# Hard-max attention on one core: key-group gathers in twos and one tile sooner throughout the loop, value gathers caught up from the sixteenth tile on

## The chip, the core and the metric

The kernel runs on one core of one Trainium2 chip. The metric is the time of one execution on the device, in microseconds (us); smaller is better. Engines are named as in the profile: PE (TensorE matmul), PEld (its weight load), DVE (VectorE), ACT (ScalarE), POOL (GpSimd), SP (SyncE). "L229" is line 229 of the kernel before.

## What is computed

```python
B, Sq, Sk, D = 4, 4096, 4096, 128
logits = np.matmul(q, k.transpose(0, 2, 1))
best = np.argmax(logits, axis=-1)
return v[b_idx, best, :]          # the value row of the best key, for every query
```

There is no softmax: each of the 16,384 query rows takes the one value row whose key has the largest product with it.

## The kernel before

**Tiles.** A tile is 128 query rows; there are 128 tiles (T = 128), 32 to a batch (NQT = 32). Iteration `it` of the main loop issues work for several tiles at different stages, and the program order of the loop is the order on each engine, since the schedule is manual.

**The screen (PE, ACT, DVE).** Keys are taken in groups of four, 1024 groups to a batch. `screen` makes four 128x1024 products in PSUM with half-precision sums and differences of keys: `dpart` (L203) has ACT take an absolute value, `spart` (L213) adds it back on PE, and ACT writes one half as E (L216). `fold` (L229) merges E with the other half on DVE into W, an integer score per group with the group's number in its low bits, and `top` (L233) takes the eight largest of 1024 on DVE. In this text the fold is called W and the max M, as their tiles W and TOP are the easiest to find in the rows. A tile costs DVE one W and one M.

**The group gather (DVE, POOL).** `gather` (L245, tile `cand`) decodes the best group's number of some tiles on DVE, and puts one indirect DMA per tile into the queue `near_q`; POOL issues it (L251, tile `kg`): it fetches the differences of the four keys of the best group, 384 half-precision numbers a row. `issue`, at the end of each iteration, takes one entry of `near_q` (two near the end).

**The dots (DVE).** `dots` waits until all gathers of its group of tiles have been issued, and some iterations more, and then multiplies kg by the query (L269, `prod`), halves the sum twice (L274 and L277, tiles `p1` and `p2`, both shown as `p`) and reduces it (L279, `D`). `pick` (L289 to L302: `mx`, `near`, `sel`, `CNT`, `win`) chooses the key for a chunk of eight tiles (four near the end).

**The value gather (POOL, SP).** `put_values` queues four indirect DMAs in `late_q`; POOL issues them (L309, tile `vr`), one or two an iteration by `take_late`, and SP stores them (L314).

**The flagged rows.** Rows whose screen was too close to call are counted and redone exactly for half of the tiles at a time: by `flag_segment` (L325 to L442) in between the loop's work from tile 64 on, and by `flags_first` and `flags_last` (L447 to L540) at the end. The last part has a branch on the count, which is not taken here.

**What sets the order.** `start` puts a generator into the list `live`; `step`, called twice an iteration, advances each by one DVE instruction: a `dots` only within a quota (one a step, two where two are waiting), a `pick` or flags generator by one. In the loop of before, an iteration is: screen, W of the tile before, `step`, M of the tile before that, `gathers` for the tile three back (from iteration TAIL = 104 on: two back), `step`, `issue`. `gathers` makes groups of four tiles for tiles 0 to 71, of two for 72 to 125, and of one for the last two. NKG is the number of kg buffers, each for four tiles.

The call that decides all of it is short:

```python
        step(it)
        if it >= 2:
            top(it - 2)
        if 3 <= it <= TAIL:
            gathers(it - 3)
        if it >= TAIL:
            gathers(it - 2)
        step(it)
        issue(it)
```

Of the kernel before, what the change touches and what calls it, by code (L numbers as in the profile page):

```python
# [8 lines left out]
FP16 = mybir.dt.float16  # L9
# [6 lines left out]
OP = mybir.AluOpType  # L16
# [5 lines left out]
TAU = 8.0  # L22
NEAR = 0.5
LATE = 7
NKG = 6


@with_exitstack
def kernel(ctx, tc, q, k, v, out):
    nc = tc.nc  # L30
    B, Sq, D = q.shape
    Sk = k.shape[1]
    P = 128
    NQT = Sq // P
    T = B * NQT
# [12 lines left out]
    rp = ctx.enter_context(tc.tile_pool(name="ref", bufs=2))  # L48
# [12 lines left out]
    natq = [bp.tile([P, NQT, P], FP16, name=f"natq{i}", tag=f"natq{i}") for i in range(2)]  # L61
# [65 lines left out]
    iota_h = cp.tile([P, P], FP16, tag="iota_h")  # L127
# [93 lines left out]
    def screen(t):  # L221
        dpart(t, 0)
        spart(t - 1, 0)
        dpart(t, 1)
        spart(t - 1, 1)
# [9 lines left out]
    fast, near_q, late_q = [], [], []  # L235
    kg_t, cand_t = {}, {}
    done, stores, marks = set(), set(), set()
    wait_q = []

    def gather(c, t0, n):  # L240
        c0, c1 = chunks[c]
        if t0 == c0:
            cand_t[c] = sp.tile([P, c1 - c0], U32, tag=f"cand{c1 - c0}", name=f"cand_{c}", bufs=6)
        x = cand_t[c][:, t0 - c0:t0 - c0 + n]
        nc.vector.tensor_scalar(out=x, in0=TOP.bitcast(U32)[:, t0:t0 + n, 0], scalar1=IDX, scalar2=IDX,  # L245
                                op0=OP.bitwise_and, op1=OP.bitwise_xor)
        kg = rp.tile([P, 4, 3, P], FP16, tag="kg", name=f"kg_{t0}", bufs=NKG)[:, 0:n]
        assert len(kg_t) < NKG
        kg_t[t0] = kg
        for j in range(n):  # L250
            near_q.append(lambda j=j: nc.gpsimd.indirect_dma_start(  # L251
                out=kg[:, j].rearrange("p f d -> p (f d)"), out_offset=None, in_=k16[t0 // NQT],
                in_offset=IOA(ap=x[:, j:j + 1], axis=0)))
        mark = lambda: done.add(("kg", t0))
        marks.add(mark)
        near_q.append(mark)
        start(dots(c, t0, n), "dots", c)

    def dots(c, x, m):
        c0 = chunks[c][0]  # L260
        d = D_t[c % 4]
        b = x // NQT
        gap = ("wait", 1) if m == 4 else ("dve",)
        yield "until", lambda: ("kg", x) in done, 2 if m < 4 and x < TAIL else 1
        kg = kg_t.pop(x)
        prod = rp.tile([P, 4, 3, P], FP16, tag="prod", name=f"prod_{x}")[:, 0:m]
        h = min(m, 2)
        for i in range(0, m, h):
            nc.vector.tensor_tensor(out=prod[:, i:i + h], in0=kg[:, i:i + h],  # L269
                                    in1=natq[b % 2][:, x + i - b * NQT:x + i + h - b * NQT, :].unsqueeze(2).to_broadcast([P, h, 3, P]),  # L270
                                    op=OP.mult)
            yield gap
        p1 = rp.tile([P, 4, 3, 64], FP16, tag="p1", name=f"p1_{x}")[:, 0:m]
        nc.vector.tensor_tensor(out=p1, in0=prod[:, :, :, 0:64], in1=prod[:, :, :, 64:128], op=OP.add)  # L274
        yield gap
        p2 = rp.tile([P, 4, 3, 32], FP16, tag="p2", name=f"p2_{x}")[:, 0:m]
        nc.vector.tensor_tensor(out=p2, in0=p1[:, :, :, 0:32], in1=p1[:, :, :, 32:64], op=OP.add)  # L277
        yield "dve",
        nc.vector.tensor_reduce(out=d[:, x - c0:x - c0 + m, 1:4], in_=p2, axis=AX_X, op=OP.add)  # L279
        done.update(("dot", i) for i in range(x, x + m))  # L280
# [40 lines left out]
    def put_rec(t0, t1):  # L321
        nc.sync.dma_start(out=rec.rearrange("(p t) w -> p t w", t=T)[:, t0:t1, :], in_=TOP.bitcast(U32)[:, t0:t1, :])
# [3 lines left out]
    def flag_segment(t0, t1, ready, stored):  # L326
# [40 lines left out]
        posn = fp.tile([P, 8], FP16, tag="posn", name=f"posn_{t0}")  # L367
        nc.vector.scalar_tensor_tensor(out=posn, in0=iota_r[:, 0:8], scalar=bs, in1=val, op0=OP.add, op1=OP.mult)
        yield "dve", 0.17
        OH = fp.tile([P, 8, P], BF16, tag="OH", name=f"OH_{t0}")  # L370
        nc.vector.tensor_tensor(out=OH, in0=iota_h.unsqueeze(1).to_broadcast([P, 8, P]),
                                in1=posn.unsqueeze(2).to_broadcast([P, 8, P]), op=OP.is_equal)
        yield "dve", 0.17
        rec2 = fp.tile([P, 8, 2], BF16, tag="rec2", name=f"rec2_{t0}")
        nc.vector.tensor_copy(out=rec2[:, :, 0], in_=e8)
        yield "dve", 0.17
# [241 lines left out]
    live = []  # L618

    def start(g, kind, c=None):  # L620
        live.append({"g": g, "kind": kind, "c": c, "wake": 0, "until": None, "n": 0})

    def ready(s, it):
        if s["until"] is not None:
            if not s["until"]():
                return False
            s["until"], s["wake"] = None, it + s["n"]
        return it >= s["wake"]

    def advance(s, it, free):  # L630
        if not (ready(s, it) or free and s["until"] is None):
            return False
        try:
            y = next(s["g"])
        except StopIteration:
            live.remove(s)
            return True
        if y[0] == "wait":
            s["wake"] = it + y[1]
        elif y[0] == "until":  # L640
            s["until"], s["n"] = y[1], y[2]
            return advance(s, it, free)
        return True

    def step(it):
        quick = it >= TAIL
        waiting = [s for s in live if s["kind"] == "dots" and ready(s, it)]
        quota = 2 if len(waiting) > 1 else 1
        for s in list(live):
            if s["kind"] == "dots":  # L650
                if quota and advance(s, it, False):
                    quota -= 1
            else:
                if advance(s, it, False) and quick and s["kind"] == "pick" and s in live:
                    advance(s, it, False)

    rest = [0]
# [1 line left out]
    def take_late(n):  # L659
        while n > 0 and late_q:  # L660
            g = late_q.pop(0)
            n -= g not in stores
            g()
        while late_q and late_q[0] in stores:
            wait_q.append((clock[0] + 2, late_q.pop(0)))
# [3 lines left out]
    def put_out(now):  # L669
        while wait_q and wait_q[0][0] <= now:  # L670
            wait_q.pop(0)[1]()

    def issue(it):
        n = 0
        clock[0] = it
        put_out(it)
        while near_q and (n < 1 + (it >= T - 28 and len(near_q) > 2) or near_q[0] in marks):
            g = near_q.pop(0)
            n += g not in marks
            g()  # L680
        if fast and it >= rest[0]:
            fast.pop(0)()
            rest[0] = it + 3
        take_late(2 if n == 0 and len(late_q) > 4 or it >= T - 24 and it % 2 == 0 else 1)

    def gathers(t):
        for c, (t0, t1) in enumerate(chunks):
            m = 4 if t1 <= T - 56 else 2 if t < T - 2 else 1
            if t0 <= t < t1 and (t - t0) % m == m - 1:
                gather(c, t - m + 1, m)  # L690
            if t == t0:
                start(pick(c, t0, t1), "pick", c)
        if t % 8 == 7:
            put_rec(t - 7, t + 1)
        if t == SEGS[1] - 1:
            last = [c for c, x in enumerate(chunks) if x[1] == t + 1][0]
            start(flag_segment(0, t + 1, lambda: ("cnt", last) in done, lambda: ("out", last) in done), "flags")

    TAIL = T - 24
    units = []  # L700
    for b in range(1, B):
        x = b * NQT
        units += [(x - 1, x - NQT + (6 + 3 * i // 2 if b == 1 else 1 + 2 * i), unit_k, b, i) for i in range(16)]
    for it in range(T):
        b, qt = it // NQT, it % NQT
        if it < 8:
            load_part(1, it)
        elif 10 <= qt < 18:
            load_part(b + 1, qt - 2)
        elif 18 <= qt < 26:  # L710
            load_part(b + 2, qt - 18)
        open_units = [u for u in units if u[1] <= it]
        if open_units:
            u = min(open_units)
            units.remove(u)
            assert it <= u[0]
            u[2](*u[3:])
        if it == 1:
            turn_q(0, 4, 8)
        if it in (1, 2, 3):  # L720
            turn_q(0, it * 8, it * 8 + 8)
        elif qt >= 16 and qt % 2 == 0 and b + 1 < B:
            turn_q(b + 1, (qt - 16) * 2, (qt - 14) * 2)
        if it > 0:
            screen(it)
        if it >= 1:
            fold(it - 1)
        if it == 1:
            put_k(0, 1)
        if it % NQT in (9, 13):  # L730
            put_k(it // NQT + 1, it % NQT // 13)
        step(it)
        if it >= 2:
            top(it - 2)
        if 3 <= it <= TAIL:
            gathers(it - 3)
        if it >= TAIL:
            gathers(it - 2)
        step(it)
        issue(it)  # L740

    def flush():
# [73 lines left out]
```

## Time and profile before

| what | value |
|---|---|
| three executions | 461.14, 462.56, 462.96 us; median 462.56 us |
| the profiled execution | 462.96 us; its span in the trace 461.1 us |
| busy share of the span | DVE 90%, PE 82%, ACT 82%, POOL 68% |
| DVE W (L229) | 128 instructions, 166.0 us |
| DVE M (L233) | 128 instructions, 156.2 us |
| DVE dots (L269, L274, L277, L279) | 65, 47, 47, 47 instructions |
| POOL gathers (L251 and L309) | 128 each, 125.7 and 134.7 us |

The span runs from the first to the last recorded instruction; the 1.9 us between it and the execution's time lie outside the trace. A record's length is not what an instruction costs its engine in a busy stretch: on DVE and ACT the next record often starts before the last one has ended. The distance from one start to the next is called the pitch here, and it is what adds up.

### The profile page before, as it was taken

To read this page: it belongs to the slowest core of one execution; us is meant where nothing else is said; L and a number is where in the kernel's file an instruction comes from. 1 tells how busy PE (TensorE), PEld (TensorE's weight loads), DVE (VectorE), ACT (ScalarE), POOL (GpSimd) and SP (SyncE) were. 2 spreads that over 40 slices of the span, in tenths; PEclk is the share of its full clock that TensorE was granted. 3 is DMA by queue.
4 is the path that set the end of the run, shared out by engine and by line. 5 is a ranking of instruction groups with operands and counts; after the bars stand their busy time and mean duration, and the time that the engine had idled before them with its cause. 6 is when DMAs were issued, how large, how long until landed. Compare 5 with 4: busy or idle time off the path is not lost. (4 is left out here: it accounts for less than half of the span.)

```text
span 461.1 us, 6319 instructions
## 1 busy us (share of the span) xinstructions
PE 380.2 (82%) x1834; PEld 168.1 (36%) x1834; DVE 414.6 (90%) x758; ACT 376.3 (82%) x437; POOL 314.3 (68%) x345
## 2 busy tenths in 40 slices
PE   8999999999998899989998889998988888850100
PEld 4444444444443344444443344433333333320100
DVE  2689999999999999899999999999999999989430
ACT  2999999999999999999999898999998887750000
POOL 8304556777667878877768877667777777777730
PEclk9999999999999999999999999999999999995555
DMA  7934657473335877843346842613333332332320
GB/s 127 199 85 96 131 91 121 76 117 86 85 97 117 163 140 113 150 95 89 88 125 139 135 122 76 132 35 83 102 104 99 87 106 78 86 94 78 96 77 4
DMA packets 43625, 47.54 MB, mean 103 GB/s; under 512 B 25001, under 2 KB 33452, under 8 KB 43585
## 3 DMA queue, kind: packets, MB, share of 16 engines
q0 software_dynamic: 18752, 30.97, 33.3%
q1 hardware_dynamic: 24832, 16.13, 13.8%
q8 instruction: 14, 0.23, 0.2%
q14 instruction: 27, 0.21, 0.2%
HBM read 39.59 MB, written 12.19 MB: 112 GB/s over the span
## 5 line engine op out<-in xcount | busy, mean ns | idle before, releaser
L203 ACT ACTIVATE A<-pd 128x1024 f16<-128x1024 f32 x256 | 259.4, 1043 | 20.5 <-PE pd L194 20.0
L251 POOL DMA_INDIRECT kg<-k,cand x128 | 125.7, 982 | 80.5 <-DVE cand L245 45.2
L229 DVE SCALAR_TENSOR_TENSOR W<-psn,E 128x1024 int16<-128x1024 f32 x128 | 166.0, 1297 | 7.8 <-ACT E L216 6.6
L194 PE MATMUL psn<-kT,qT 128*128 128x512 f16 x512 | 151.9, 378 | 16.3 <-ACT A L203 7.1
L194 PE MATMUL pd<-kT,qT 128*128 128x512 f16 x512 | 151.8, 378 | 13.0 <-ACT A L203 11.3
L309 POOL DMA_INDIRECT vr<-in_v_dram,win x128 | 134.7, 1053 | 40.3 <-issue 35.6
L194 PEld LDWEIGHTS <-qT 128*128 128x128 f16 x1024 | 98.0, 97 | 162.5 <-issue 74.3
L233 DVE MAX8 TOP<-W 128x8 f32<-128x1024 f32 x128 | 156.2, 1220 | 0.0
L213 PE MATMUL psn<-A,identh 128*128 128x512 f16 x512 | 152.1, 378 | 0.0
L216 ACT ACTIVATE E<-psn 128x1024 int16<-128x1024 f32 x128 | 132.3, 1033 | 4.2 <-PE psn L213 4.2
L213 PEld LDWEIGHTS <-identh 128*128 128x128 f16 x512 | 49.6, 97 | 60.8
L269 DVE TENSOR_TENSOR prod<-kg,natq 128x768 f16<-128x768 f16 (+1 forms) x65 | 35.3, 543 | 3.0 <-DMA kg<-k,cand 3.0
L174 ACT ACTIVATE kT<-uk 128x256 f16<-128x256 f32 x48 | 20.4, 424 | 1.4 <-PE uk L171 1.4
L274 DVE TENSOR_TENSOR p<-prod 128x384 f16<-128x384 f16 (+2 forms) x47 | 20.0, 426 | 0.1
L279 DVE TENSOR_REDUCE D<-p 128x6 f32<-128x192 f16 (+2 forms) x47 | 19.7, 419 | 0.1
L65 POOL DMA_DIRECT2D natk<-in_k_dram x27 | 16.0, 600 | 0.8 <-POOLq L800 0.8
L68 POOL DMA_DIRECT2D natq<-in_q_dram x27 | 16.2, 603 | 0.0
L170 PE MATMUL uk<-identh,natk 128*128 128x128 f16 x96 | 15.8, 218 | 0.0
L469 PE MATMUL fp_e<-n_e,tri 128*128 128x1 f32 x2 | 0.6, 362 | 16.4 <-DVE n_e L467 16.4
L277 DVE TENSOR_TENSOR p<-p 128x192 f16<-128x192 f16 (+2 forms) x47 | 13.5, 287 | 0.1
L171 PEld LDWEIGHTS <-natk 128*128 128x128 f16 x96 | 9.3, 97 | 7.0 <-issue 4.5
L170 PEld LDWEIGHTS <-natk 128*128 128x128 f16 x96 | 9.4, 98 | 5.6
(147 smaller groups left out, 131.5 us busy)
## 6 DMA issues: line engine op xcount, KB each, us to landing
out_dram<-vr SPq DMA_DIRECT2D x32, 256.0 KB, 2.2
natq<-in_q_dram POOLq DMA_DIRECT2D x26, 128.0 KB
k<-kd SPq DMA_DIRECT2D x8, 384.0 KB, 2.9
natk<-in_k_dram POOLq DMA_DIRECT2D x24, 128.0 KB
kg<-k,cand POOLq DMA_INDIRECT x128
vr<-in_v_dram,win POOLq DMA_INDIRECT x128
natq<-in_q_dram POOLq DMA_DIRECT2D x1, 768.0 KB
natk<-in_k_dram POOLq DMA_DIRECT2D x1, 512.0 KB
```

Source lines behind the costliest of these rows:

```text
L170: nc.tensor.matmul(out=o, lhsT=natk[b % 2][:, h, 4 * m + x, :], rhs=identh, start=True, stop=False)
L174: nc.scalar.activation(out=kT[b % 2][:, c:c + 256], in_=ps, func=AF.Copy)
L194: nc.tensor.matmul(out=ps[:, n * 512:(n + 1) * 512], lhsT=qT[b % 2][:, qt * P:(qt + 1) * P], rhs=kT[b % 2][:, u * 1024 + n * 512:u * 1024 ...
L203: nc.scalar.activation(out=A, in_=ps, func=AF.Abs)
L213: nc.tensor.matmul(out=ps[:, n * 512:(n + 1) * 512], lhsT=identh, rhs=A[:, n * 512:(n + 1) * 512], start=False, stop=True)
L216: nc.scalar.activation(out=E, in_=ps, func=AF.Relu, scale=QSCALE)
L229: nc.vector.scalar_tensor_tensor(out=W_t[t % NW].bitcast(I16)[:, 1::2], in0=ps, scalar=QSCALE, in1=E, op0=OP.mult, op1=OP.max)
L233: nc.vector.max(out=TOP[:, t, :], in_=W_t[t % NW].bitcast(FP32))
L251: near_q.append(lambda j=j: nc.gpsimd.indirect_dma_start(out=kg[:, j].rearrange("p f d -> p (f d)"), out_offset=None, in_=k16[t0 // NQT], ...
L269: nc.vector.tensor_tensor(out=prod[:, i:i + h], in0=kg[:, i:i + h], in1=natq[b % 2][:, x + i - b * NQT:x + i + h - b * NQT, :].unsqueeze(2 ...
L274: nc.vector.tensor_tensor(out=p1, in0=prod[:, :, :, 0:64], in1=prod[:, :, :, 64:128], op=OP.add)
L309: late_q.append(lambda j=j: nc.gpsimd.indirect_dma_start(out=vr[:, j, :], out_offset=None, in_=v_flat, in_offset=IOA(ap=win[:, i + j:i + j ...
```

## The change

The change does seven things, all in the order of the work: (1) groups are of two tiles for tiles 0 to 125, with eight kg buffers of two tiles in place of six of four; (2) `gathers` always works two tiles back, and after the second `step` in place of before it; (3) `dots` yields as "dve" alone, and waits two iterations after its gathers up to TAIL, one from there on; TAIL is 90 in place of 104; (4) `issue` takes two entries of `near_q` wherever more than three wait; (5) `issue` takes a second value gather wherever more than eight wait and it is every third iteration (and when more than three wait with no group gather taken, or in the last 28 iterations); (6) a flags generator is advanced twice a step, and picks twice from the new TAIL on; (7) the one-hot comparison of `flag_segment` is cut into four instructions, an iteration apart.

```diff
-NKG = 6
...
-        kg = rp.tile([P, 4, 3, P], FP16, tag="kg", name=f"kg_{t0}", bufs=NKG)[:, 0:n]
-        assert len(kg_t) < NKG
+        kg = rp.tile([P, 2, 3, P], FP16, tag="kg", name=f"kg_{t0}", bufs=8)[:, 0:n]
+        assert len(kg_t) < 8
...
-        gap = ("wait", 1) if m == 4 else ("dve",)
-        yield "until", lambda: ("kg", x) in done, 2 if m < 4 and x < TAIL else 1
+        yield "until", lambda: ("kg", x) in done, 1 if x >= TAIL else 2
...
-        h = min(m, 2)
-        for i in range(0, m, h):
-            nc.vector.tensor_tensor(out=prod[:, i:i + h], in0=kg[:, i:i + h],
...
-            yield gap
+        nc.vector.tensor_tensor(out=prod, in0=kg, in1=natq[b % 2][:, x - b * NQT:x - b * NQT + m, :].unsqueeze(2).to_broadcast([P, m, 3, P]),
+                                op=OP.mult)
+        yield "dve",
...
-        nc.vector.tensor_tensor(out=OH, in0=iota_h.unsqueeze(1).to_broadcast([P, 8, P]),
-                                in1=posn.unsqueeze(2).to_broadcast([P, 8, P]), op=OP.is_equal)
-        yield "dve", 0.17
+        for z in range(4):
+            nc.vector.tensor_tensor(out=OH[:, 2 * z:2 * z + 2], in0=iota_h.unsqueeze(1).to_broadcast([P, 2, P]),
+                                    in1=posn[:, 2 * z:2 * z + 2].unsqueeze(2).to_broadcast([P, 2, P]), op=OP.is_equal)
+            yield "wait", 1
...
-                if advance(s, it, False) and quick and s["kind"] == "pick" and s in live:
+                if advance(s, it, False) and (quick or s["kind"] == "flags") and s in live:
...
-        while near_q and (n < 1 + (it >= T - 28 and len(near_q) > 2) or near_q[0] in marks):
+        behind = len(near_q) > 3
+        while near_q and (n < 1 + behind or near_q[0] in marks):
...
+            n += 1
-        take_late(2 if n == 0 and len(late_q) > 4 or it >= T - 24 and it % 2 == 0 else 1)
+        left = len([g for g in late_q if g not in stores])
+        more = n == 0 and left > 3 or n < 2 and it % 3 == 0 and left > (8 if it < T - 28 else 3)
+        take_late(2 if more else 1)
...
-            m = 4 if t1 <= T - 56 else 2 if t < T - 2 else 1
+            m = 2 if t < T - 2 else 1
...
-    TAIL = T - 24
+    TAIL = T - 38
...
         step(it)
         if it >= 2:
             top(it - 2)
-        if 3 <= it <= TAIL:
-            gathers(it - 3)
-        if it >= TAIL:
+        step(it)
+        if it >= 2:
             gathers(it - 2)
-        step(it)
         issue(it)
```

More of the change, by code (lines that the diff above doesn't have):

```diff
@@ L262, in dots @@
         b = x // NQT
-        gap = ("wait", 1) if m == 4 else ("dve",)
-        yield "until", lambda: ("kg", x) in done, 2 if m < 4 and x < TAIL else 1
+        yield "until", lambda: ("kg", x) in done, 1 if x >= TAIL else 2
         kg = kg_t.pop(x)
-        prod = rp.tile([P, 4, 3, P], FP16, tag="prod", name=f"prod_{x}")[:, 0:m]
-        h = min(m, 2)
-        for i in range(0, m, h):
-            nc.vector.tensor_tensor(out=prod[:, i:i + h], in0=kg[:, i:i + h],
-                                    in1=natq[b % 2][:, x + i - b * NQT:x + i + h - b * NQT, :].unsqueeze(2).to_broadcast([P, h, 3, P]),
-                                    op=OP.mult)
-            yield gap
-        p1 = rp.tile([P, 4, 3, 64], FP16, tag="p1", name=f"p1_{x}")[:, 0:m]
+        prod = rp.tile([P, 2, 3, P], FP16, tag="prod", name=f"prod_{x}")[:, 0:m]
+        nc.vector.tensor_tensor(out=prod, in0=kg, in1=natq[b % 2][:, x - b * NQT:x - b * NQT + m, :].unsqueeze(2).to_broadcast([P, m, 3, P]),
+                                op=OP.mult)
+        yield "dve",
+        p1 = rp.tile([P, 2, 3, 64], FP16, tag="p1", name=f"p1_{x}")[:, 0:m]
         nc.vector.tensor_tensor(out=p1, in0=prod[:, :, :, 0:64], in1=prod[:, :, :, 64:128], op=OP.add)
-        yield gap
-        p2 = rp.tile([P, 4, 3, 32], FP16, tag="p2", name=f"p2_{x}")[:, 0:m]
+        yield "dve",
+        p2 = rp.tile([P, 2, 3, 32], FP16, tag="p2", name=f"p2_{x}")[:, 0:m]
         nc.vector.tensor_tensor(out=p2, in0=p1[:, :, :, 0:32], in1=p1[:, :, :, 32:64], op=OP.add)
```

## The prediction

> **What bounds the kernel now.** First the page's busy shares and its slices. DVE's slices read 9 from the third to the 35th; ACT's and PE's sink to 8 in the last third.
>
> ```profile
> span 461.1 us, 6319 instructions
> PE 380.2 (82%) x1834; PEld 168.1 (36%) x1834; DVE 414.6 (90%) x758; ACT 376.3 (82%) x437; POOL 314.3 (68%) x345
> DVE  2689999999999999899999999999999999989430
> ```
>
> Busy records overlap, so I went on to DVE's timeline and took pitches, from one start to the next. Here are two iterations with groups of four, and two with groups of two:
>
> ```profile
> 105.17 0.16 DVE L245 TENSOR_SCALAR cand<-TOP 128x4 uint32<-128x4 uint32 x1
> 105.22 0.55 DVE L279 TENSOR_REDUCE D<-p 128x12 f32<-128x384 f16 x1
> 105.69 1.30 DVE L229 SCALAR_TENSOR_TENSOR W<-psn,E 128x1024 int16<-128x1024 f32 x1
> 106.88 0.56 DVE L269 TENSOR_TENSOR prod<-kg,natq 128x768 f16<-128x768 f16 x1
> 107.36 1.21 DVE L233 MAX8 TOP<-W 128x8 f32<-128x1024 f32 x1
> 108.50 1.28 DVE L229 SCALAR_TENSOR_TENSOR W<-psn,E 128x1024 int16<-128x1024 f32 x1
> ```
> ```profile
> 302.94 0.26 DVE L245 TENSOR_SCALAR cand<-TOP 128x2 uint32<-128x2 uint32 x1
> 303.00 0.39 DVE L274 TENSOR_TENSOR p<-prod 128x384 f16<-128x384 f16 x1
> 303.27 1.33 DVE L229 SCALAR_TENSOR_TENSOR W<-psn,E 128x1024 int16<-128x1024 f32 x1
> 304.47 0.27 DVE L277 TENSOR_TENSOR p<-p 128x192 f16<-128x192 f16 x1
> 304.63 1.25 DVE L233 MAX8 TOP<-W 128x8 f32<-128x1024 f32 x1
> 305.77 0.36 DVE L279 TENSOR_REDUCE D<-p 128x6 f32<-128x192 f16 x1
> 306.02 1.33 DVE L229 SCALAR_TENSOR_TENSOR W<-psn,E 128x1024 int16<-128x1024 f32 x1
> ```
>
> W takes 1.19 of pitch and M 1.14, whoever follows, and the next record begins some 0.085 before the last one ends. From W of tile 12 (52.16) to W of tile 126 (411.05) the pitches of all of DVE's instructions, each form at its mean, add up to 355.8 of 358.9 us, and three waits below are the other 3.0: DVE is the bound. ACT's own three activations a tile have a pitch of 0.91 each, 2.73, and a kT copy 0.3; a tile of DVE takes 2.92 with groups of four. What interrupts DVE there is one row of the view of waits; the first row is from the start of the loop:
>
> ```profile
> DVE W L229 <- ACT E L216: 6.6, 9, 2.8
> DVE prod L269 <- DMA kg<-k,cand: 3.0, 3, 1.4
> ```
>
> The three waits for kg are 1.40 us at 193, 0.28 at 360 and 1.31 at 407. The last: POOL's gather of that group ended at 406.9, its `prod` began at 408.9, so a gather is usable some 2.0 after its record. In the end part (from W of tile 126 at 411.05) DVE and POOL work through one chain to 461.1.
>
> **The change, part by part.** The built orders of both kernels, side by side, give 75 more DVE instructions and the same number on the other engines. From W of tile 126 on, DVE's order is the same but for one swapped pair, and POOL's from the gather of tile 122 on: the end part does not change. So the sum is over DVE's stretch before it.
>
> *A, groups of two for 72 tiles: +5.2.* A group of four cost prod 2 x 0.467, p1 0.466, p2 0.262, reduction 0.463, cand 0.06 = 2.19. Two groups of two, by the pitches of tiles 72 up, cost 2 x (0.467 + 0.267 + 0.168 + 0.264 + 0.07) = 2.47. 18 groups times 0.28 to 0.30 make 5.0 to 5.4. In the new order cand stands ahead of W, which the trace shows only where W was late anyway (0.18 of pitch); other short ones ahead of W (`near`, `CNT`) cost 0.085 to 0.09, so I keep 0.07 and let 0.18 stretch the range: at most 4 to 5 us more over some 45 such places.
> The Trainium skill, "VectorE: DVE Perf Modes", in the section on the TRN2 errata, speaks against this part: a fixed extra time is paid once per instruction, so large tiles are better than many small ones; its table has 58 cycles at 0.96 GHz, 60 ns, as the fixed part. By that, 72 more instructions would cost an estimated 4.3 in place of 5.2; the rows (p1: 2 x 0.267 - 0.466 = 0.068) win.
>
> *B, the one-hot in four: +0.25.* 1024 elements had a pitch of 1.12 (L371), 512 one of 0.60 (L480); along that line 256 have 0.34, four of them 1.37.
>
> *C, dots sooner: -2.2.* DVE's twelve iterations from W of tile 0 (16.64) to W of tile 12 (52.16) took 35.5, but their pitches add up to 29.6 (12 W, 11 M, two kd of 0.86, two prod, two cand): 5.9 idle, behind ACT's E. In the new order five cand, three prod and three sets of p1, p2 and reduction stand there, 3.0 more work, which is not done later. Stepping through from 34.05 by pitches (3.13 and 2.76 in turn, kd on two of them), never ahead of before's ACT-bound starts, I get W of tile 12 at 52.6 and W of tile 14 0.4 later than before's 58.92. So 3.0 are moved and 0.4 lost; since DVE's lateness also holds ACT's buffers I take 0.8. Bounds: gain 2.8, or none at all, if ACT loses as much as DVE puts in.
>
> *D, cand no longer directly behind its own M: -1.4.* From tile 104 on before works two tiles back, and cand directly behind M started 1.26 after it, not 1.14. Twelve such places, times 0.12. In the new order a `step` stands between; those of the end part stay.
>
> *E, picks and flags two at a time: +1.2.* Where one instruction reads what the last one wrote, its start is 0.035 behind the record's end, not 0.085 ahead: 0.12 each. The built order has ten more such pairs (eight of flags, two of picks).
> On D and E the same page, in "The DRAIN you can't avoid", says that a semaphore between two VectorE operations costs nothing extra. By that rule D and E would both be zero, and the sum 0.2 higher; this trace says otherwise, 1.26 against 1.14.
>
> *F, waits for kg: -3.0 + 1.6.* Before's three go. New ones can come: POOL is in order, pitch 1.26 for a kg and 1.31 for a vr, so an iteration with one of each takes 2.57, a third vr every third iteration 0.43 more, a q or k load 0.61: 3.0 to 3.6 for an iteration of 3.0. While loads run, `prod` stands four iterations behind cand, three whole ones and a W, 10 us, and POOL needs 0.4 + 2 x 1.26 + 2 x 1.31 + 0.6 + 2.0 = 8.1: enough. From tile 90 on it stands three behind. Around tile 106 two flag transfers (FV and the store of its rows) and a second vr stand between the two gathers of a group: 0.4 + 2 x 1.26 + 3 x 1.31 + 2.0 = 8.9 for about 7.8 (two iterations of 3.3 and a W). One to two us there, less than one for the group after. Against that the new order has 52 transfers on POOL between the gathers of tiles 100 and 122, before 58. Bounds: no wait at all, or 4.
>
> *Rest.* SP's queue has the same transfers; transposes of the next batch have over ten iterations of slack. PE and ACT do the same work and have 0.1 to 0.25 a tile to spare. The end part loses one pair of D, -0.1.
>
> *Sum.* 5.2 + 0.25 - 2.2 - 1.4 + 1.2 - 3.0 + 1.6 - 0.1 = +1.6. The profiled execution took 462.96 (461.1 of span and 1.9 around it), so by its own time 464.5. It is the longest of the three; against their median of 462.56 I forecast **464.2**.
>
> **Rivals.** About 0.5%, 2.3 us, is what a measurement of this kernel can tell from no change.
>
> 1. *POOL becomes the bound (slower).* Value gathers taken ahead push group gathers back, and with TAIL at 90 there are 14 more iterations in which `prod` has one iteration less of room. It decides once POOL is more than 0.6 us further behind than I reckon, as each group then waits. Five to seven waits of 0.7 on tiles 90 to 112 make 4 in place of 1.6: 467. For it: the waits at 360 and 407 came in just such a place. Against it: fewer transfers are left there.
> 2. *The small instructions cost more (slower).* If cand ahead of W costs 0.13 rather than 0.07 and early ACT loses what DVE puts in, 1.6 + 2.7 + 0.8: 467.5; half of it 466.
> 3. *The fill works better (faster).* C gives 2.8, no wait for kg is left, and flag pairs are not held: 5.0 + 0.25 - 2.8 - 1.4 + 0.2 - 3.0 - 0.1 = -1.8, and if ACT too runs ahead for the better in the first batch, another 1: 460. For it: before has three waits, each near POOL's limit.
> 4. *The catching up does nothing.* The end part has the same order on POOL and DVE, and POOL there waits for DVE (0.98 idle ahead of FR, the flagged rows' first gather, at 430.7): the value gathers left over are the same 11. So none of the sum is put on them; that is part of the forecast.
>
> **How the numbers follow.** Forecast case, within 0.5%, 464.2: chance 0.50; its own range 462 to 465. Rival 1: 0.28. Rival 2: 0.10. Rival 3: 0.12. So faster by over 0.5% 0.12, within 0.5% 0.50, slower 0.38. The range of eight in ten goes from 461.2, which leaves out most of rival 3, to 467.2, which leaves out the far part of rivals 1 and 2.
>
> **What would show it.** A: a chunk of eight tiles in the first 70 takes 24.0 on DVE and not 23.4. C: first `prod` near 38 and not 46.7, W of tile 14 at 59.3 to 59.8. D: no 1.26 behind M from tile 104 on. F: the row of `prod` waiting for kg has 1 to 2 us, around tile 106, and none near 193. End part: 50 us from W of tile 126 to the end of the span, as before. I am wrong if W starts late behind ACT after tile 20, if cand's pitch ahead of W is over 0.1, or if that row is over 3.

## The result, and the profile after

The changed kernel takes 466.71 us (median; 466.19 to 467.09), the kernel before beside it 462.37 (461.14 to 462.96): ratio 1.0097, interval [1.0074, 1.0120]. It is 4.3 us slower; 464.2 was forecast, with 461.2 to 467.2 as the range. The time lies in the range, but the likeliest case, within 0.5%, did not come; a slower one did.

The two profiled executions, 462.96 before and 466.19 after, lie only 3.2 apart: before's was the longest of its three first runs, and after's the shortest of its own. What the traces can explain is 3.2; the other 1.1 lies in how executions scatter.

The changed kernel's page, its busy shares and DVE's 40 slices:

```profile
span 464.4 us, 6400 instructions
...
PE 381.8 (82%) x1834; PEld 168.5 (36%) x1834; DVE 419.0 (90%) x833; ACT 377.7 (81%) x437; POOL 316.2 (68%) x345
...
DVE  2689999999999999899999999999999899999530
```

DVE has 75 instructions and 4.4 us of records more, at the same share of 90%, and its slices read 9 for longer. The page alone shows only that DVE is still the bound. DVE's rows in the view of waits say more (engine, what waited, for what: us in all, times, longest):

```profile
DVE W L228 <- ACT E L215: 4.1, 4, 2.8
DVE prod L265 <- DMA kg<-k,cand: 3.7, 5, 1.3
DVE W L228 <- PE psn L212: 1.6, 3, 0.7
```

The first row, again all from the start of the loop, has fallen from 6.6: the dots fill some of it. The second was to fall from 3.0 to between 1 and 2, and rose to 3.7. That is the row over 3 by which the prediction said it would be wrong.

From one W past the next in DVE's timeline (start, length, then line, operation, tiles), the new order with pairs:

```profile
113.18 1.30 DVE L228 SCALAR_TENSOR_TENSOR W<-psn,E 128x1024 int16<-128x1024 f32 x1
114.37 0.17 DVE L297 SCALAR_TENSOR_TENSOR win<-CNT,cand 128x8 uint32<-128x8 f32 x1
114.44 0.56 DVE L265 TENSOR_TENSOR prod<-kg,natq 128x768 f16<-128x768 f16 x1
114.91 1.23 DVE L232 MAX8 TOP<-W 128x8 f32<-128x1024 f32 x1
116.04 0.35 DVE L269 TENSOR_TENSOR p<-prod 128x384 f16<-128x384 f16 x1
116.30 0.17 DVE L244 TENSOR_SCALAR cand<-TOP 128x2 uint32<-128x2 uint32 x1
116.37 1.32 DVE L228 SCALAR_TENSOR_TENSOR W<-psn,E 128x1024 int16<-128x1024 f32 x1
```

`cand` to W is 0.07 of pitch, as was taken, and no 0.12 is lost behind M (114.91 to 116.04 is 1.13).

The whole account by W's starts: W of tile 14 begins at 58.92 before and 59.09 after; W of tile 126 at 411.05 and 414.70, 3.65 later; from there to the end of the span 50.06 and 49.65. Of the 3.65, the waits on DVE in tiles 12 to 125, taken as pitch beyond an instruction's normal one, are 1.4 (3.25 before, 4.61 after) and the work itself 2.3. Before's 3.25 are all for kg. Of the 4.61 after, 4.2 are for kg, and 0.4 is a W that waits for PE's `psn` at 175.

The waits for kg stand in two places. The first is the load stretch, where q and k of later batches are fetched (16 loads on POOL, from 144 to 194). DVE's timeline there:

```profile
187.03 1.30 DVE L228 SCALAR_TENSOR_TENSOR W<-psn,E 128x1024 int16<-128x1024 f32 x1
188.23 0.15 DVE L297 SCALAR_TENSOR_TENSOR win<-CNT,cand 128x8 uint32<-128x8 f32 x1
189.17 0.56 DVE L265 TENSOR_TENSOR prod<-kg,natq 128x768 f16<-128x768 f16 x1 [0.79 <-DMA kg<-k,cand]
```

and POOL's:

```profile
181.64 0.98 POOL L250 DMA_INDIRECT kg<-k,cand  x1 [0.30 <-DMA kg<-k,cand]
182.93 1.01 POOL L304 DMA_INDIRECT vr<-in_v_dram,win  x1 [0.31 <-issue]
183.94 0.60 POOL L64 DMA_DIRECT2D natk<-in_k_dram  x1
184.85 0.98 POOL L250 DMA_INDIRECT kg<-k,cand  x1 [0.30 <-issue]
186.14 1.01 POOL L304 DMA_INDIRECT vr<-in_v_dram,win  x1 [0.30 <-issue]
187.15 0.60 POOL L64 DMA_DIRECT2D natk<-in_k_dram  x1
188.06 0.99 POOL L250 DMA_INDIRECT kg<-k,cand  x1 [0.30 <-issue]
```

From kg to kg POOL takes 3.21, and a tile of DVE with pairs 2.99: POOL falls behind by 0.2 a tile for as long as the loads go on. The `cand` of the group that is waited for (tiles 50 and 51) began at 178.0. Its first gather started 3.7 later (1.0 later for the group of tile 40, up to 4.0 for that of tile 52), its second ended at 185.83, and `prod` could start 3.34 after that: 11.2 in all, where DVE's own order leaves about 10.3. This wait and the next, at 196, are 1.7 of pitch. In before the same lag was there, with groups of four: for tiles 48 to 51 (two lines of DVE and two of POOL)

```profile
177.10 0.14 DVE L245 TENSOR_SCALAR cand<-TOP 128x4 uint32<-128x4 uint32 x1
181.14 0.98 POOL L251 DMA_INDIRECT kg<-k,cand  x1 [0.30 <-DMA kg<-k,cand]
...
191.17 0.99 POOL L251 DMA_INDIRECT kg<-k,cand  x1 [0.30 <-issue]
194.79 0.56 DVE L269 TENSOR_TENSOR prod<-kg,natq 128x768 f16<-128x768 f16 x1 [1.40 <-DMA kg<-k,cand]
```

the first gather starts 4.0 behind `cand`, the last ends at 192.16, and the second `prod` starts 2.6 after that.

The second place is from W of tile 97 to W of tile 113, 2.5 of pitch. There `prod` of the group of tile 94 waits 0.7: TAIL at 90 leaves it three iterations and not four. The groups of tiles 106 and 108 wait 1.7 together. They have three iterations in before too, and the group of tile 106 waits 0.4 there; but from its `cand` to where DVE's own order puts `prod` it has 9.2 in before and 7.9 after. That `gathers` now stands behind the second `step` is a likely reason.

### The profile page after: what moved, and what is told of

Read it like the earlier page. It is cut to its first block, busy times and chain, and to the rows that moved or that the text cites. A ratio compares the mean times of both kernels' runs of the same rounds, so it can differ in the third digit from the quotient of the medians.

```text
span 464.4 us, 6400 instructions
## 1 busy us (share of the span) xinstructions
PE 381.8 (82%) x1834; PEld 168.5 (36%) x1834; DVE 419.0 (90%) x833; ACT 377.7 (81%) x437; POOL 316.2 (68%) x345
## 5 line engine op out<-in xcount | busy, mean ns | idle before, releaser
L212 PEld LDWEIGHTS <-identh 128*128 128x128 f16 x512 | 49.6, 97 | 60.8
L269 DVE TENSOR_TENSOR p<-prod 128x384 f16<-128x384 f16 (+1 forms) x65 | 22.5, 347 | 0.1
L274 DVE TENSOR_REDUCE D<-p 128x6 f32<-128x192 f16 (+1 forms) x65 | 22.2, 342 | 0.1
L272 DVE TENSOR_TENSOR p<-p 128x192 f16<-128x192 f16 (+1 forms) x65 | 16.4, 253 | 0.1
L170 PEld LDWEIGHTS <-natk 128*128 128x128 f16 x96 | 9.3, 97 | 7.4 <-issue 4.7
L244 DVE TENSOR_SCALAR cand<-TOP 128x2 uint32<-128x2 uint32 (+1 forms) x65 | 11.7, 180 | 0.1
```

Source lines behind the costliest of these rows:

```text
L212: nc.tensor.matmul(out=ps[:, n * 512:(n + 1) * 512], lhsT=identh, rhs=A[:, n * 512:(n + 1) * 512], start=False, stop=True)
```

## Experiments

**Theory, after the traces:** POOL is so nearly full in the load stretch, and leaves so little room from TAIL on, that DVE's `prod` waits for it; the rest is the pairs' own instructions. **Rivals:** the value gathers taken ahead push the group gathers back (a cause that the prediction's rival 1 gave); or the small flag instructions are what costs.

This table has all twelve runs, for comparison in the text below. "Waits" are those on DVE in tiles 12 to 125, as pitch; "work" is the start of W of tile 126 less these waits; "end" is from there to the end of the span. The last three are from the one profiled execution, in us. Two executions differ in such waits by some 0.3 even where the orders are the same (e2 below).

| kernel | median | ratio to before, interval | waits | work | end |
|---|---|---|---|---|---|
| before | 462.4 | 1 | 3.2 | 407.8 | 50.1 |
| after | 466.71 | 1.0097 [1.0074, 1.0120] | 4.6 | 410.1 | 49.7 |
| e3 pairs alone | 466.78 | 1.0106 [1.0087, 1.0126] | 4.0 | 410.6 | 49.9 |
| e11 sooner, groups as before | 462.20 | 1.0013 [0.9999, 1.0026] | 5.2 | 405.5 | 49.7 |
| e4 after with fours | 461.33 | 0.9985 [0.9971, 0.9999] | 4.0 | 406.5 | 49.7 |
| e1 more room | 464.29 | 1.0046 [1.0032, 1.0059] | 2.6 | 410.1 | 49.8 |
| e8 value gathers held | 469.35 | 1.0152 [1.0133, 1.0170] | 7.9 | 409.9 | 49.7 |
| e2 no catching up | 467.79 | 1.0119 [1.0104, 1.0134] | 5.9 | 410.1 | 50.1 |
| e6 flags once a step | 464.02 | 1.0034 [1.0022, 1.0045] | 4.4 | 409.2 | 49.7 |
| e12 e4, flags once | 464.02 | 1.0043 [1.0024, 1.0062] | 5.7 | 405.6 | 49.6 |
| e5 e4, more room | 465.39 | 1.0054 [1.0040, 1.0068] | 1.3 | 409.9 | 52.4 |
| e7 put together | 465.11 | 1.0048 [1.0034, 1.0062] | 1.0 | 407.0 | 55.2 |
| e9 e7, caught up faster | 461.06 | 0.9976 [0.9967, 0.9985] | 1.9 | 407.3 | 49.7 |
| e10 e9, less room | 464.65 | 1.0053 [1.0038, 1.0067] | 6.1 | 406.9 | 49.7 |

### The halves: pairs, and sooner

e3 is before with groups of two throughout and nothing else:

```diff
-NKG = 6
+NKG = 8
...
-            m = 4 if t1 <= T - 56 else 2 if t < T - 2 else 1
+            m = 2 if t < T - 2 else 1
```

(with tiles kg, prod, p1 and p2 for two tiles in place of four.)

> The kernel before, with groups of two tiles throughout and eight buffers, and nothing else of the change. Theory: 18 groups times 0.28 us of pitch (measured in the profile after: 23.92 to 23.38 us for eight tiles, 0.54) is 4.9 more on DVE; dots start three iterations earlier (iteration of tile 7, not 10), which fills some 2 us of DVE's idle time behind ACT; before's wait of 1.4 near 193 us goes or stays: 464 to 466. Rival, the grouping is free and the rest of the change costs the 4.3: 462.4.

Measured 466.78: the pairs alone cost as much as the whole change. Their work is 2.8 more. Two waits for kg stand where before has three, the longest of 2.0:

```profile
core 0 of [0], span 464.6 us
...
DVE prod L269 <- DMA kg<-k,cand: 2.7, 2, 2.0
```

The other 1.2 of its waits are W behind PE's `psn` (three times, from 175 to 276). No `prod` waits in the load stretch here: there the first gather starts at most 2.8 after its `cand`, against 4.0 in the changed kernel.

e4 is the other way round, the changed kernel with fours for tiles 0 to 71:

```diff
-            m = 2 if t < T - 2 else 1
+            m = 4 if t1 <= T - 56 else 2 if t < T - 2 else 1
```

(and six buffers and the dots of before for four tiles.)

> The kernel after, with groups of four for tiles 0 to 71 as before had them, and all else as after. Theory: DVE gets 4.9 us back, loses some 1.5 of the early fill (first multiplication at tile 9, not 6), and the waits after 319 us stay (2.4): 462.5 to 464.5. Rival, the grouping is free: 466 to 467.

Measured 461.33, 5.4 less than the changed kernel and 1.2 below the lower end of what was expected; by the traces 3.6 of that is work and 0.7 waits. e11 is before with the order of the loop, the new TAIL and the dots' rule of waiting. Other than its expectation says, it also has the changed kernel's rule for a second group gather:

```diff
-        yield "until", lambda: ("kg", x) in done, 2 if m < 4 and x < TAIL else 1
+        yield "until", lambda: ("kg", x) in done, 1 if x >= TAIL else 2
...
-        while near_q and (n < 1 + (it >= T - 28 and len(near_q) > 2) or near_q[0] in marks):
+        behind = len(near_q) > 3
+        while near_q and (n < 1 + behind or near_q[0] in marks):
...
-    TAIL = T - 24
+    TAIL = T - 38
...
-        if 3 <= it <= TAIL:
-            gathers(it - 3)
-        if it >= TAIL:
-            gathers(it - 2)
         step(it)
+        if it >= 2:
+            gathers(it - 2)
```

> The kernel before with only the group gathers a tile sooner in the whole loop, after the second step (and TAIL at 90, with dots two iterations after their gathers up to there): groups stay at four, flags are advanced once a step, the one-hot is one instruction, and the queues' rules are those of before. By the terms measured so far: the dots sooner take 2.0 off, the decoding behind M 1.3; waits for the group gathers as in the kernel with fours, 4.0 of pitch for 3.25, plus 1 to 1.4 without the catching up: 460.0 to 461.8 us. If the pairs were not the only part that costs, and the sooner gathers cost too (POOL then has less time for each group of four), waits of over 6 us and 463 or more.

Measured 462.20, above the expectation by 0.4 and not to be told from before. Its work is 2.3 less, where C and D together were reckoned at 3.6, and its waits give 1.9 of that back:

```profile
core 0 of [0], span 460.4 us
...
DVE prod L268 <- DMA kg<-k,cand: 4.5, 4, 3.0
```

So sooner gathers do free DVE, and DVE then waits for POOL. How much of these waits comes from the rule for a second group gather was not run.

### Where the waits come from

e1 gives `prod` an iteration more of room in the changed kernel, up to tile 111:

```diff
-        yield "until", lambda: ("kg", x) in done, 1 if x >= TAIL else 2
+        yield "until", lambda: ("kg", x) in done, 3 if x < TAIL else 2 if x < 112 else 1
```

> The kernel after, with one more iteration between the gathers of a group and its first multiplication (three in place of two before tile 90, two in place of one from 90 to 111). Theory, DVE's pitches add up and its waits for kg (4.4 us of pitch above normal in the profile after: 2.0 at 174 to 194 us, 2.4 from 319 to 375) are only a lack of room: at most 0.5 us of them is left, dots begin one iteration later in the first batch, which gives back 0.5 to 1, so 463.0 (462.3 to 463.8) where after has 466.7. Rival, POOL is the bound in those stretches: the waits move with the order and 3 to 5 us are left, 466 to 467.

Measured 464.29, 2.4 below the changed kernel, where 3.7 had been expected. Of the five waits for kg one is left, that of the group of tile 112, which has no more room than in the changed kernel:

```profile
core 0 of [0], span 462.4 us
...
DVE W L228 <- PE psn L212: 2.2, 4, 0.7
DVE prod L265 <- DMA kg<-k,cand: 1.3, 1, 1.3
```

Work is as in the changed kernel, 410.1, and the 2.0 that go are waits. That is what room is worth; the 2.3 of work over before stay.

e8 takes the value gathers out of every second iteration of the load stretches, and so makes room on POOL itself:

```diff
-        take_late(2 if more else 1)
+        b, qt = it // NQT, it % NQT
+        load = 10 <= qt < 18 and b + 1 < B or 18 <= qt < 26 and b + 2 < B
+        take_late(0 if load and it % 2 == 0 else 2 if more else 1)
```

> The kernel after, with no value gather in every second iteration in which a load of q or k is issued (they are taken later instead). Theory: POOL falls behind in the 17 iterations with loads, as kg 1.28 + vr 1.30 + load 0.61 = 3.2 us is over an iteration's 3.0; with every second vr left out it is 2.55 on average, so the waits of 0.88 and 0.82 at 188 and 194 us go, and those after 319 us stay or grow by up to 1: 465.0 (464.3 to 466.3). Rival, those two waits come from the landing of kg among the loads' own traffic: they stay, 466.7.

Measured 469.35: the wrong sign. In the load stretch it did what the theory says: the first gather starts 0.4 to 0.7 behind its `cand` at tiles 48 to 54 (3.4 to 4.0 in the changed kernel), and of the 1.7 of waits there 0.2 are left. Slow landing among the loads, the rival, does not go (a gather of the group of tile 48 can be used only 4.5 after its record), so what e8 took away is POOL's lag. But the gathers that were held come back, and waits from 312 to 378 grow to 7.3:

```profile
core 0 of [0], span 467.5 us
...
DVE prod L265 <- DMA kg<-k,cand: 6.7, 7, 2.2
```

What had been missed: POOL has nothing to spare later either, once `prod` has only three iterations.

e2 leaves out the catching up and keeps all the rest:

```diff
-        left = len([g for g in late_q if g not in stores])
-        more = n == 0 and left > 3 or n < 2 and it % 3 == 0 and left > (8 if it < T - 28 else 3)
-        take_late(2 if more else 1)
+        take_late(2 if n == 0 and len(late_q) > 4 or it >= T - 24 and it % 2 == 0 else 1)
```

> The kernel after, with before's rule for how many value gathers POOL takes (no catching up at every third iteration). Theory, the waits come from where the first multiplication stands: the two near 190 us stay or shrink by at most a half, the ones after 319 us stay between 1 and 4 us in all, 465 to 468. Rival, the value gathers taken ahead push the group gathers back: all waits but 0.5 us go and the time is 462.5 to 463.

Measured 467.79, slower and not faster:

```profile
core 0 of [0], span 466.1 us
...
DVE prod L265 <- DMA kg<-k,cand: 4.5, 8, 1.2
```

Up to 320 us (W of tile 97) POOL's order is the same in the two kernels: the new rule takes nothing ahead of before's rule there, although it is meant to from the sixteenth tile on, and cannot be what made the waits of the load stretch (2.0 here and 1.7 in the changed kernel, which is how far two executions differ). Behind 320 the orders differ, and the waits after tile 95 grow from 2.5 to 3.4. So it is not the catching up that holds up the group gathers; without it, things are worse. This rival falls. Value gathers as such do take POOL's time, as e8 shows in the load stretch.

### The small instructions

e6 advances flags once a step again and leaves the one-hot whole, in the changed kernel; e12 does the same to e4:

```diff
-        for z in range(4):
-            nc.vector.tensor_tensor(out=OH[:, 2 * z:2 * z + 2], in0=iota_h.unsqueeze(1).to_broadcast([P, 2, P]),
-                                    in1=posn[:, 2 * z:2 * z + 2].unsqueeze(2).to_broadcast([P, 2, P]), op=OP.is_equal)
-            yield "wait", 1
+        nc.vector.tensor_tensor(out=OH, in0=iota_h.unsqueeze(1).to_broadcast([P, 8, P]),
+                                in1=posn.unsqueeze(2).to_broadcast([P, 8, P]), op=OP.is_equal)
+        yield "dve", 0.17
...
-                if advance(s, it, False) and (quick or s["kind"] == "flags") and s in live:
+                if advance(s, it, False) and quick and s["kind"] == "pick" and s in live:
```

> The kernel after, with flags advanced once a step and the one-hot in one instruction, as before. Theory of the prediction, a DVE instruction that reads what the one just before it wrote starts 0.12 us later than another (eight such pairs go), and three one-hot instructions go: 1.2 us less of pitch, 465.5, give or take 1 for waits for kg, which the trace tells apart. Rival, the semaphore between two DVE instructions costs nothing: 0.25 less of pitch, 466.5.

> As e11, with the catching up of the value gathers and the second group gather wherever more than three wait, as in the changed kernel. If the catching up alone is a gain: 0.8 to 1.4 us below e11, 459.0 to 460.5. If it only moves waits from the last third of the loop to the load stretch: within 0.5 us of e11.

e6: 464.02, 2.7 below the changed kernel; in the traces W of tile 126 is 1.05 sooner, 0.9 of it work. The other 1.6 is not in the profiled execution, which was among e6's longer ones (465.08). e12: 464.02, 2.7 above e4, and 1.8 above e11, where a gain or no difference had been expected. Its work is 1.0 less than e4's, and its waits are 1.7 more; these 0.7 are in the traces, while the other 2.0 of the medians are not (its profiled execution, 462.67, is the second shortest of seven). So the same edit is worth 2.7 in one company and costs 2.7 in the other: it saves about as much work on DVE in both (0.9 and 1.0), and the waits, and what the traces do not show, decide. Differences of single parts do not add up here. The sign of the queue rules is no more fixed than that of the flags: the catching up is a gain of 1.1 in the changed kernel (e2), and a loss of 1.8 between e11 and e12. These two kernels differ in it alone; the second group gather, which e12's expectation names as well, is in both, and DVE's order is the same in both.

### Putting it together, and a path not seen before

e5 is e4 with more room; e7 has more of the kind: pairs for tiles 0 to 7 alone (to fill the start), fours up to 71, flags and one-hot as in e6. Both have

```diff
-        yield "until", lambda: ("kg", x) in done, 1 if x >= TAIL else 2
+        yield "until", lambda: ("kg", x) in done, 3 if m == 4 else 2 if x < 110 else 1
```

> The kernel after with groups of four for tiles 0 to 71, and more room between gathers and the first multiplication: three iterations for groups of four, two for groups of two up to tile 109, then one. Theory, DVE's pitches add up and waits are lack of room: of the 3.95 us of waits that the same kernel had without the room at most 1.5 are left, the longer way costs 0.5 in the first batch: 459.0 (458.0 to 460.0) where without the room it took 461.3. Rival, POOL is the bound and room only moves the waits: 461 to 462.

> What the theory would make of both kernels: after's order of an iteration and its catching up of value gathers; groups of two in the first eight tiles, where DVE waits for ACT anyway, of four up to tile 71, of two from there; three iterations of room for the fours, two for the twos of tiles 72 to 109; flags once a step, one-hot in one. Theory: 459.0 of the kernel with fours and room, less 1.2 for flags and one-hot, less 0.5 for the first eight tiles: 457.3 (456 to 459). Rival, POOL is the bound: 461 or more.

Both missed by far on the wrong side, 465.39 and 465.11, though the waits did what was expected: hardly any, and in e7 none for kg at all.

Part of the miss is work. e5 has 3.4 more of it than e4, as the room for groups of four puts their `cand` directly behind its M again, which is the 1.26 of part D:

```profile
113.43 1.23 DVE L232 MAX8 TOP<-W 128x8 f32<-128x1024 f32 x1
114.70 0.17 DVE L244 TENSOR_SCALAR cand<-TOP 128x4 uint32<-128x4 uint32 x1
```

There are 16 such places in e5, 2.0 at 0.12 to 0.13 each, and 15 in e7, e9 and e10; e4, e11 and the changed kernel have none from W of tile 12 to W of tile 126. This cost is still in e9 below.

The rest is lost in the end part: 52.4 in e5 and 55.2 in e7 for 50, though DVE was through with its last instruction at 439.78 in e7, against 443.14 before. POOL's timeline of e7 there (the three FK gathers end at 435.29, then):

```profile
443.57 1.00 POOL L308 DMA_INDIRECT vr<-in_v_dram,win  x1 [0.31 <-issue]
449.48 0.99 POOL L502 DMA_INDIRECT FV<-in_v_dram,xw_fe  x1 [4.92 <-DMA vr<-in_v_dram,win]
452.16 1.03 POOL L539 DMA_INDIRECT out_dram<-FV,rowk_e  x1 [1.69 <-DMA FV<-in_v_dram,xw_fe]
```

With more room the picks, and so the value gathers, come later; 15 are left at the end of the loop, seven of them behind FK, where before has 11 and three. The branch on the count stands behind the last of them on POOL, and FV starts 4.9 after that one's end, though DVE had ended 9.7 before. e9 only makes the catching up faster, so that 11 are left again:

```diff
-        more = n == 0 and left > 3 or n < 2 and it % 3 == 0 and left > (8 if it < T - 28 else 3)
+        more = n == 0 and left > 1 or n < 2 and (it % 2 == 0 if it >= 72 else it % 3 == 0) and left > (8 if it < 72 else 2)
```

> The kernel of e7 (fours in the load stretch, flags once a step, groups gathered a batch of dots earlier) with only the catching up of the value gathers made faster, so that 11 of them are left at the end of the loop, as in the kernel before, and not 15. If the branch on POOL behind the last value gather is what took e7's 3.4 us away, VectorE ends near 440 us as in e7 (443.14 before), the flagged gathers start 4 to 5 us later, and the run is 459.0 to 460.8 us. If instead POOL has no room for three or four more value gathers in the loop, they come back as waits of prod for the group gathers: more than 3 us of such waits behind tile 97, VectorE's end past 442 and 462 us or more.

Measured 461.06: 4.1 less than e7, and faster than before by 0.24%, interval [0.9967, 0.9985]. The expectation is missed by 0.3, but its point holds: DVE ends at 440.60, 0.8 later than in e7, and FV starts 4.4 sooner.

```profile
439.13 1.09 POOL L308 DMA_INDIRECT vr<-in_v_dram,win  x1 [0.30 <-issue]
445.06 0.99 POOL L502 DMA_INDIRECT FV<-in_v_dram,xw_fe  x1 [4.84 <-DMA vr<-in_v_dram,win]
```

Four value gathers of 1.30 less are 5.2, and its FK ends 0.8 later: 4.4. In the kernels before, after, e4, e7, e9, e11 and e12 the gap between the end of the last value gather and FV is 4.84 to 4.96 in each, while DVE's last instruction ends anywhere from 4.8 before that gather's end to 0.8 after it. The view of waits names the branch (L580) ahead of FV in before, and that last gather's own transfer in e7. FV's time follows POOL's last gather, then, and not DVE's end.

e10 is e9 with the faster catching up from tile 100 only, and an iteration of room less for tiles 104 to 109 (`2 if x < 104 else 1`):

> As e9, with the catching up at one more in two tiles from tile 100 only, and the dots of tiles 104 to 109 a tile sooner again (room for one tile less), so that the picks, and with them the last value gathers, come sooner. Theory of the branch: within 0.8 us of e9, 459.0 to 461.0, since the value gathers left are again 11. If VectorE waits for the group gathers in these tiles, as it did in the changed kernel at tiles 106 to 112, about 1.3 us for each group more: 461 to 463, and the waits stand between 365 and 385 us.

Measured 464.65, neither of the two. VectorE does wait for group gathers, but from 324 to 358, 5.3 of pitch, ahead of the place named.

```profile
core 0 of [0], span 462.8 us
...
DVE prod L268 <- DMA kg<-k,cand: 4.8, 3, 3.0
```

The groups of tiles 94 to 102 wait 2.2 of it. Their room is as in e9, so these waits come with the catching up, which is slower than e9's from 72 to 99. The group of tile 104 waits 3.1; it has both edits, and which of them brings that is open.

## Why the prediction was wrong where it was

**A, pairs: right.** A chunk of eight tiles takes 23.92 on DVE, where 24.0 was forecast and 23.38 is before's: 0.54 more, for 0.56 to 0.60 by the rows. `cand` ahead of W is 0.07, and ACT keeps up after tile 20, so rival 2 fell.

**B and E, one-hot and pairs of flags: about right.** 1.45 was forecast for both. e6 undoes the one-hot and eight of the ten pairs, 1.2 of it, and has 0.9 less work in the trace. The Trainium skill, "VectorE: DVE Perf Modes", in "The DRAIN you can't avoid", has a semaphore between two operations cost nothing extra; by that rule e6 would show the 0.25 of B alone. The 0.9 lies between, nearer to the 1.2 of the rows.

**C, dots sooner: better than reckoned.** The first `prod` starts at 35.1 (near 38 was forecast), and W of tile 14 is 0.17 late and not 0.4 to 0.8. Some of C turned out to belong to the pairs: in e3, too, tiles 72 to 125 have 1.8 less work, since more dots are done by then.

**D: right.** No 1.26 behind M in tiles 104 to 125 (before has eleven such places ahead of W of tile 126, not twelve), and the work of tiles 72 to 125 is 2.9 less than before's, most of it C and D.

Without F and the end part the sum was +3.05; the traces have +2.3.

**F, waits for kg: the step that failed.** "Before's three go", and 1.6 come: -1.4. Measured: 4.2 of waits for kg, 1.0 more than before, a miss of 2.4. Together with the 0.4 of W behind `psn`, which "Rest" put at nothing, and less the 0.7 of work and 0.3 of end part that came out better, this is, but for rounding, the gap of 1.7 between the forecast sum (1.55, unrounded) and the two traces (3.24). In the load stretch the prediction set "8.1: enough" against 10. It took a group by itself: a first gather 0.4 behind `cand`, and a gather usable 2.0 after its record. Measured in the group at 189 are 3.7 and 3.3; the part between (4.2 against 5.7) was reckoned too high. The 3.7 is backlog: the prediction itself had 3.0 to 3.6 for POOL's iteration against DVE's 3.0, and did not add up the difference over 16 loads. Both were in sight: before's group of tile 48 shows 4.0 and 2.6 (the lines above), and the 2.0 was taken from the one at 407, where no loads run. From TAIL on the price was right for the groups of tiles 106 and 108 (1.7 of pitch, "one to two us"), but the group of tile 94 adds 0.7.

**The rivals.** Rival 1 had the right engine and nearly the right size (4 in place of 1.6; 4.2), but put all of it behind tile 90, where 2.5 stand, and named the value gathers taken ahead, which e2 refutes. Its other reason, TAIL at 90, holds for 0.7. e1 shows that room takes the waits away, and e8 that those of the load stretch come from POOL's lag. Rival 4 holds as far as it went: 11 value gathers were left in both, and the end part, forecast 50, took 49.65. But the reason it gave, that POOL "waits for DVE", is only true ahead of FR; e7 and e9 show that the number left is on the path.

**The rest of the gap.** The forecast was put 0.36 below its own sum for the median of before, and the change's executions lie up to 0.9 above its profiled one. The traces do not explain the 1.1 by which the medians lie further apart than the profiled executions. That the time still lies in the range is owed to the upper end, which was set for rivals 1 and 2, and not to the terms of the forecast case.

## What to carry to other kernels

Where an in-order engine serves the bound one, compare their periods over the whole stretch in which they differ, and not one iteration's latency with its room: 0.2 a tile over 16 loads made 1.7 of waits here where none were forecast. What is saved on the bound engine turns into waits if the engine beside it is nearly as full; the sign of an edit then depends on its company, and taking "work" and "waits" apart shows what it does, as far as the traces go. Count what is queued ahead of a branch or barrier on every engine, the idle-looking ones too.

## What had not been expected of the hardware

- **When an indirect gather can be used.** From the end of a kg's record (128 rows of 768 bytes) to the start of the `prod` that waited for it: 1.65 to 2.1 in most such places of the last third of the loop, 2.4 to 4.5 in the load stretch of eight kernels (before 2.6, after 3.3 and 3.4, e4 3.9, e6 4.1, e8 4.5, e12 2.4 among them), and 2.7 to 3.8 in six places without loads (e2 328, e3 358, e4 324, e5 397, e8 363, e11 356). The loads' transfers are a likely cause in the one place, not shown; in the other it is open. The Trainium skill, "DMA: Bandwidth & Descriptors", in "Anatomy of one DMA", fits 2.0 us plus bytes over 436e3; for these 98,304 bytes that is an estimated 2.2. The 1.65 to 2.1 here come near it; the 2.4 to 4.5 and 2.7 to 3.8 lie above.
- **The branch.** From the end of POOL's last gather to its first transfer behind the branch, 4.84 to 4.96 us pass with nothing recorded on POOL. In after, e9 and e11 the view of DMA issues has that gather land 2.5 to 2.6 after its start, some 1.5 after its record's end. What fills the other 3.3, no run here shows. The three value gathers between FK and the branch are 3.9 us of POOL ahead of it in before, after and e9; taking them sooner, so that the branch stands behind FK, was not tried.
